# Binary cross entropy of 8192x8192 on one core: a side block of 24 rows, loaded by part of the DMA engines at launch and near the end, and chunks of 13824 columns

## The chip, the core and the metric

The kernel runs on one core of one Trainium2 chip. The core has several engines that run their own instruction streams: VectorE (DVE in the profile), ScalarE (ACT), GpSimd (POOL), SyncE (SP) and TensorE (PE, which has no work here). Sixteen DMA engines move data between HBM and the on-chip memory of 128 partitions. Transfers are issued by SP or by POOL; the profile lists SP's as queue q1 (hardware_dynamic) and POOL's as q0 (software_dynamic).

The metric is the time of one execution on the device in microseconds (us). The kernel before takes 1865.45 us, the median of three runs (1865.32 to 1865.6).

## The reference

```python
def reference(pred, target):                     # both 8192 x 8192, float32
    eps = 1e-7
    pred = np.clip(pred, eps, 1 - eps)
    return -(target * np.log(pred) + (1 - target) * np.log(1 - pred))
```

The predictions lie between 0.01 and 0.99. The target is 0 or 1 in every element, so the result is -log|target - 1 + pred|: for target 1 this is -log(pred), for target 0 it is -log(1 - pred). The kernel computes it in that form. Two arrays of 268 MB are read from HBM and one of 268 MB is written.

## The kernel before, in words

The three arrays are taken as flat and cut into chunks. A chunk of w columns is 128 x w consecutive elements, one partition holding w of them. The 524288 columns are cut by `plan` into two chunks of 5120 (`FIRST`), 35 of 14336 (`BIG`), two of 5632 (`LAST`) and one of 1024 (`TAIL`): 40 chunks.

Two tiles hold the data. `ring_p` (float32) has three slots of `BIG` columns and a place for the last chunk; pred is loaded into it, everything is computed in place, and the result is stored from it. `ring_t` (bf16) has one slot of `BIG` columns and a place for the last chunk; the target is loaded into it by a transfer that casts float32 to bf16. As there is one slot, the target of chunk k+1 can be loaded only when DVE has read all of the target of chunk k.

The work on a chunk, in halves for the large ones, is:

- `clip` (L80): DVE, tensor_scalar, clamps pred to [eps, 1-eps]
- `log`: first DVE (L86, scalar_tensor_tensor: target - 1 + pred), then ACT twice (L89 absolute value, L90 logarithm)
- `back` (L94): DVE, tensor_scalar, times -1
- `store` (L76): a transfer from `ring_p` to the output

`load_p` (L69) and `load_t` (L72) are issued on POOL, as are the stores, with these exceptions on SP: the pred load of chunk 0, and the stores of the last three chunks. One transfer of a chunk has 128 rows, one for each partition. Each DMA engine takes eight of them, one after the other, and works through what has been issued in the order of its queues.

The order is written out by hand (`tc.manual_schedule`), and each engine runs its instructions in that order. At launch POOL issues the target loads of chunks 0 and 1 and the pred loads of chunks 1 and 2, SP the pred load of chunk 0. After DVE has worked on chunks 0 and 1, POOL issues the target load of chunk 2, then the stores of chunks 0 and 1 and the pred load of chunk 3. From then on one round of the loop over k computes chunk k, issues the target load of chunk k+1 (when the second L86 of chunk k is done), the store of chunk k (when the second L94 is done), and the pred load of chunk k+2. The last three chunks are interleaved by hand.

The semaphores are put in by the framework from the data that instructions touch. POOL's transfers use eight semaphores in turn, so that a transfer of POOL also waits until the one issued eight before it has landed.

Of the kernel before, what the change touches and what calls it, by code (L numbers as in the profile page):

```python
# [1 line left out]

# [4 lines left out]

EPS = 1e-7

BIG = 14 * 1024  # L10
FIRST = 5 * 1024
LAST = 5632
TAIL = 1024
SLOTS = 3


def plan(total):
    n = (total - 2 * FIRST - 2 * LAST - TAIL) // BIG
    assert n > 4 and total == 2 * FIRST + n * BIG + 2 * LAST + TAIL
    spots = [(FIRST, 0, 0), (FIRST, FIRST, FIRST)]  # L20
    spots += [(BIG, k % SLOTS * BIG, 0) for k in range(1, n + 1)]
    end = (n + 1) % SLOTS * BIG
    spots += [(LAST, end, 0), (LAST, end + LAST, LAST)]
    return spots + [(TAIL, SLOTS * BIG, BIG)]


@with_exitstack
def kernel(
    ctx: ExitStack,
    tc: tile.TileContext,  # L30
    pred: bass.AP,
    target: bass.AP,
    out: bass.AP,
):
    nc = tc.nc
    fp32 = mybir.dt.float32
    bf16 = mybir.dt.bfloat16
    Alu = mybir.AluOpType
    Act = mybir.ActivationFunctionType
    P = nc.NUM_PARTITIONS  # L40

    R, C = pred.shape
    spots = plan(R * C // P)
    n = len(spots)
    widths = [s[0] for s in spots]
    cols = [sum(widths[:k]) for k in range(n)]

    def chunk(ap, k):
        flat = ap.rearrange("r c -> (r c)")
        return flat[cols[k] * P : (cols[k] + widths[k]) * P].rearrange("(p w) -> p w", p=P)  # L50

    pool = ctx.enter_context(tc.tile_pool(name="rings", bufs=1))
    ring_p = pool.tile([P, SLOTS * BIG + TAIL], fp32, name="ring_p", tag="ring_p")
    ring_t = pool.tile([P, BIG + TAIL], bf16, name="ring_t", tag="ring_t")
    warm = pool.tile([1, 8], fp32, name="warm", tag="warm")

    def spot(k, part=(0, 1)):
        w, c, _ = spots[k]
        i, m = part
        return ring_p[:, c + i * w // m : c + (i + 1) * w // m]  # L60

    def spot_t(k, part=(0, 1)):
        w, _, c = spots[k]
        i, m = part
        return ring_t[:, c + i * w // m : c + (i + 1) * w // m]

    def load_p(k):
        queue = nc.sync if k == 0 else nc.gpsimd
        queue.dma_start(out=spot(k), in_=chunk(pred, k))  # L69

    def load_t(k):
        nc.gpsimd.dma_start(out=spot_t(k), in_=chunk(target, k))  # L72

    def store(k):
        queue = nc.sync if k >= n - 3 else nc.gpsimd
        queue.dma_start(out=chunk(out, k), in_=spot(k))  # L76

    def clip(k, *part):
        p = spot(k, *part)
        nc.vector.tensor_scalar(  # L80
            out=p, in0=p, scalar1=EPS, scalar2=1 - EPS, op0=Alu.max, op1=Alu.min
        )

    def log(k, *part):
        p = spot(k, *part)
        nc.vector.scalar_tensor_tensor(  # L86
            out=p, in0=spot_t(k, *part), scalar=1.0, in1=p, op0=Alu.subtract, op1=Alu.add
        )
        nc.scalar.activation(out=p, in_=p, func=Act.Abs)  # L89
        nc.scalar.activation(out=p, in_=p, func=Act.Ln)  # L90

    def back(k, *part):
        p = spot(k, *part)
        nc.vector.tensor_scalar(out=p, in0=p, scalar1=-1.0, scalar2=None, op0=Alu.mult)  # L94

    with tc.manual_schedule():
        nc.vector.memset(warm, 1.0)  # L97
        load_t(0)
        load_p(0)
        load_t(1)  # L100
        load_p(1)
        load_p(2)
        nc.scalar.activation(out=warm, in_=warm, func=Act.Ln)  # L103
        for k in (0, 1):
            clip(k)
            log(k)
        load_t(2)
        back(0)
        store(0)
        back(1)  # L110
        store(1)
        load_p(3)
        a, b, c = range(n - 3, n)
        for k in range(2, n - 3):
            for h in (0, 1):
                clip(k, (h, 2))
                log(k, (h, 2))
            if k < n - 4:
                load_t(k + 1)
            else:  # L120
                load_t(a)
                load_t(b)
                load_p(c)
                load_t(c)
                back(k, (0, 2))
                for j in (a, b):
                    clip(j)
            if k < n - 4:
                back(k, (0, 2))
            back(k, (1, 2))  # L130
            store(k)
            if k + 2 < n - 3:
                load_p(k + 2)
            elif k + 2 == n - 3:
                load_p(a)
                load_p(b)
        log(a, (0, 2))
        log(a, (1, 2))
        clip(c)
        log(b, (0, 2))  # L140
        back(a, (0, 2))
        log(b, (1, 2))
        back(a, (1, 2))
        store(a)
        log(c)
        back(b, (0, 2))
        back(b, (1, 2))
        store(b)
        back(c)
        store(c)  # L150


# [1 line left out]
_INS = ['pred', 'target']  # L154
_OUTS = [((8192, 8192), 'float32')]


# [23 lines left out]
```

## Time and profile before

| what | before |
|---|---|
| median of three runs | 1865.45 us |
| the profiled execution | 1865.98 us |
| its span, first to last instruction | 1864.2 us |
| DVE busy | 1121.5 us (60%) |
| ACT busy | 902.4 us (48%) |
| POOL busy | 178.4 us (10%) |
| HBM read, written | 536.87 MB, 268.44 MB |
| L86 on 128x7168, 70 times | 7.625 us each |
| L89, L90 on 128x7168, 70 times each | 6.17, 6.18 us each |
| L80, L94 on 128x7168, 70 times each | 3.89 us each |
| L72 on POOL waits for DVE's L86 | 1057.4 us in all, 37 times |
| L86 on DVE waits for the target's transfer | 371.9 us in all, 35 times |
| large target load, issue to landing | 31.3 us (median of 35) |
| large pred load, issue to landing | 44.3 us (median of 35) |
| large store, issue to landing | 31.1 us (median of 35) |

Times of instructions are from the start of the span. An engine's busy time is the sum of its instructions; the profile puts the idle time ahead of an instruction down to what ended it. The DMA share of a stretch is the mean over the sixteen DMA engines; in short stretches it can come out a few per cent above 1 or below the true share. The profile has no number for a DMA engine, but it has the start and length of every packet, and packets that follow each other without a gap can be joined into sixteen chains. "Target chunk 2" and the like count chunks from 0, as `k` does.

### The profile page before, as it was taken

The page shows a single profiled execution, that of the slowest core. Times are in us where ns is not written, and L with a number is a line of the kernel's source. Part 1 is how long each engine was busy: PE and PEld are TensorE (multiplying, and loading weights), DVE is VectorE, ACT ScalarE, POOL GpSimd, SP SyncE. Part 2 cuts the span into 40 slices and gives each one's busy share as a digit, 9 for nine tenths or more (in the row PEclk, how much of TensorE's full clock was granted, in tenths as well). Part 3 has the DMA queues.
Part 4 walks back from the last instruction along what each step waited for, and adds up shares of the span by engine and source line. Part 5 has one row for each costly group of instructions (what it writes and reads, how often), then busy time and mean ns, then how long its engine had stood idle before and what let it go on. Part 6 is the DMA issues. An engine that isn't in the chain of part 4 may idle for free.

```text
span 1864.2 us, 704 instructions
## 1 busy us (share of the span) xinstructions
DVE 1121.5 (60%) x230; ACT 902.4 (48%) x156; POOL 178.4 (10%) x120
## 2 busy tenths in 40 slices
DVE  4666555555666566555555666566655555666565
ACT  4454444455555544444455555544444445555554
POOL 1111101111110011101111110011101111110020
DMA  9999999999999999999999999999999999999999
GB/s 345 346 371 356 354 354 353 354 354 356 357 374 373 375 372 354 354 354 356 359 356 359 357 368 375 376 373 362 353 354 354 356 354 354 356 367 374 374 357 348
DMA packets 17286, 671.15 MB, mean 360 GB/s; under 512 B 1920, under 2 KB 1920, under 8 KB 2304
## 3 DMA queue, kind: packets, MB, share of 16 engines
q0 software_dynamic: 16704, 662.18, 99.0%
q1 hardware_dynamic: 576, 8.91, 1.1%
q14 instruction: 6, 0.05, 0.0%
HBM read 536.87 MB, written 268.44 MB: 432 GB/s over the span
## 4 chain that ended last, share of the span: by engine, by line
DMA 60%; issue 35%; ACT 3%; DVE 2%; POOL 0%; POOLq 0%; DVEq 0%; PEldq 0%
DMA ring_t<-in_target_dram 57%; DMA ring_p<-in_pred_dram 4%; ACT ring_p L90 1%; ACT ring_p L89 1%; DVE ring_p L86 1%; DVE ring_p L94 0%; DVE ring_p L80 0%; POOL out_dram L76 0%; POOL ring_t L72 0%; POOLq L72 0%; POOL ring_p L69 0%; POOLq L76 0%; DVEq L86 0%; PEldq L176 0%
## 5 line engine op out<-in xcount | busy, mean ns | idle before, releaser
L89 ACT ACTIVATE ring_p<-ring_p 128x7168 f32<-128x7168 f32 (+3 forms) x77 | 452.0, 5870 | 942.7 <-DVE ring_p L86 942.7
L86 DVE SCALAR_TENSOR_TENSOR ring_p<-ring_t,ring_p 128x7168 f32<-128x7168 bf16 (+3 forms) x77 | 558.2, 7251 | 373.2 <-DMA ring_t<-in_target_dram 371.9
L94 DVE TENSOR_SCALAR ring_p<-ring_p 128x7168 f32<-128x7168 f32 (+3 forms) x77 | 285.4, 3706 | 329.5 <-ACT ring_p L90 329.5
L90 ACT ACTIVATE ring_p<-ring_p 128x7168 f32<-128x7168 f32 (+3 forms) x77 | 452.6, 5877 | 2.5
L80 DVE TENSOR_SCALAR ring_p<-ring_p 128x7168 f32<-128x7168 f32 (+3 forms) x75 | 284.5, 3794 | 23.9 <-DMA ring_p<-in_pred_dram 23.9
L76 POOL DMA_DIRECT2D out_dram<-ring_p x37 | 127.9, 3458 | 584.5 <-DVE ring_p L94 584.3
L72 POOL DMA_DIRECT2D ring_t<-in_target_dram x40 | 28.9, 722 | 1058.2 <-DVE ring_p L86 1057.4
L69 POOL DMA_DIRECT2D ring_p<-in_pred_dram x39 | 21.7, 558 | 2.5 <-issue 2.5
L103 ACT ACT_TABLE_LOAD x1 | 1.3, 1283 | 0.7 <-PEq L165 0.7
L97 DVE MEMSET warm<- 1x8 f32 x1 | 0.1, 65 | 0.8 <-PEq L165 0.8
L103 ACT ACTIVATE warm<-warm 1x8 f32<-1x8 f32 x1 | 0.2, 208 | 0.0
L165 POOL MEMSET const-float32-0.0<- 128x1 f32 x1 | 0.1, 98 | 0.2 <-issue 0.2
L165 POOL MEMSET const-bfloat16-1.0<- 128x1 bf16 x1 | 0.1, 101 | 0.0
L165 POOL MEMSET const-float32-1.0<- 128x1 f32 x1 | 0.1, 98 | 0.0
L165 POOL MEMSET const-uint8-127<- 128x1 uint8 x1 | 0.1, 98 | 0.0
## 6 DMA issues: line engine op xcount, KB each, us to landing
ring_p<-in_pred_dram POOLq DMA_DIRECT2D x35, 7168.0 KB, 44.3
out_dram<-ring_p POOLq DMA_DIRECT2D x35, 7168.0 KB, 31.1
ring_t<-in_target_dram POOLq DMA_DIRECT2D x35, 3584.0 KB, 31.3
ring_p<-in_pred_dram POOLq DMA_DIRECT2D x2, 2816.0 KB, 37.2
out_dram<-ring_p SPq DMA_DIRECT2D x2, 2816.0 KB, 14.7
out_dram<-ring_p POOLq DMA_DIRECT2D x2, 2560.0 KB, 28.7
ring_t<-in_target_dram POOLq DMA_DIRECT2D x2, 1408.0 KB, 26.5
ring_p<-in_pred_dram SPq DMA_DIRECT2D x1, 2560.0 KB, 13.0
```

The costliest lines, as they stand in the source:

```text
L69: queue.dma_start(out=spot(k), in_=chunk(pred, k))
L72: nc.gpsimd.dma_start(out=spot_t(k), in_=chunk(target, k))
L76: queue.dma_start(out=chunk(out, k), in_=spot(k))
L80: nc.vector.tensor_scalar(out=p, in0=p, scalar1=EPS, scalar2=1 - EPS, op0=Alu.max, op1=Alu.min)
L86: nc.vector.scalar_tensor_tensor(out=p, in0=spot_t(k, *part), scalar=1.0, in1=p, op0=Alu.subtract, op1=Alu.add)
L89: nc.scalar.activation(out=p, in_=p, func=Act.Abs)
L90: nc.scalar.activation(out=p, in_=p, func=Act.Ln)
L94: nc.vector.tensor_scalar(out=p, in0=p, scalar1=-1.0, scalar2=None, op0=Alu.mult)
L97: nc.vector.memset(warm, 1.0)
L103: nc.scalar.activation(out=warm, in_=warm, func=Act.Ln)
L165: nc = _bacc.Bacc("TRN2", target_bir_lowering=False, num_devices=1)
```

## The change

The sizes of the chunks change: 36 chunks of 13824 columns (not 35 of 14336), two first ones of 6912 (not 5120), two of 5632 as before, and a last one of 948 (not 1024). The remaining 588 columns' worth of data, 75264 elements of each array, form a side block in two tiles of their own, `side_p` and `side_t`, both float32.

The side block has a low and a high part. The low part is 24 rows of 2x800 elements, in groups of 12, 8 and 4 rows (`GROUPS`). Its target and pred are loaded by six transfers that SP issues at launch, behind the pred load of chunk 0. The high part is the complement: 4, 8 and 12 rows (16 less the group) of 2x768 elements. POOL loads its target at k = n-13 and its pred at k = n-12, and stores the result at k = n-8. The low part's result is computed at k = 4 and stored by POOL in three pieces of 384, 384 and 32 columns at k = n-13, n-12 and n-8. Here n is the number of chunks, 41. Each group has the partitions j, j+9, j+18 and so on for the low part, and 3+j, 12+j and so on for the high one, so that no partition is shared.

Both parts are computed by DVE and ACT on all 128 partitions of the side tiles, 1600 columns at k = 4 and 1536 at k = n-9, with the same five operations as a chunk. Two memsets of DVE fill the side tiles at launch, so that partitions that no transfer fills hold numbers.

```diff
--- before.py
+++ after.py
@@ -7,16 +7,20 @@
 
 EPS = 1e-7
 
-BIG = 14 * 1024
-FIRST = 5 * 1024
+BIG = 108 * 128
+FIRST = BIG // 2
 LAST = 5632
-TAIL = 1024
+TAIL = 948
 SLOTS = 3
+HALF = 800
+CUT = 768
+GROUPS = [12, 8, 4]
+SIDE = 24 * 2 * (HALF + CUT) // 128
 
 
 def plan(total):
-    n = (total - 2 * FIRST - 2 * LAST - TAIL) // BIG
-    assert n > 4 and total == 2 * FIRST + n * BIG + 2 * LAST + TAIL
+    n = (total - 2 * FIRST - 2 * LAST - TAIL - SIDE) // BIG
+    assert n > 12 and total == 2 * FIRST + n * BIG + 2 * LAST + TAIL + SIDE
     spots = [(FIRST, 0, 0), (FIRST, FIRST, FIRST)]
     spots += [(BIG, k % SLOTS * BIG, 0) for k in range(1, n + 1)]
     end = (n + 1) % SLOTS * BIG
@@ -52,7 +56,29 @@
     pool = ctx.enter_context(tc.tile_pool(name="rings", bufs=1))
     ring_p = pool.tile([P, SLOTS * BIG + TAIL], fp32, name="ring_p", tag="ring_p")
     ring_t = pool.tile([P, BIG + TAIL], bf16, name="ring_t", tag="ring_t")
+    side_p = pool.tile([P, 2, HALF], fp32, name="side_p", tag="side_p")
+    side_t = pool.tile([P, 2, HALF], fp32, name="side_t", tag="side_t")
     warm = pool.tile([1, 8], fp32, name="warm", tag="warm")
+    low_cols = sum(widths) * P
+    high_cols = low_cols + sum(GROUPS) * 2 * HALF
+
+    def low(ap, j, a, b):
+        flat = ap.rearrange("r c -> (r c)")
+        at = low_cols + sum(GROUPS[:j]) * 2 * HALF
+        block = flat[at : at + GROUPS[j] * 2 * HALF]
+        return block.rearrange("(h p w) -> p h w", h=2, w=HALF)[:, :, a:b]
+
+    def low_rows(tile_, j, a, b):
+        return tile_[j : j + 9 * GROUPS[j] - 8 : 9, :, a:b]
+
+    def high(ap, j):
+        flat = ap.rearrange("r c -> (r c)")
+        at = high_cols + sum(16 - g for g in GROUPS[:j]) * 2 * CUT
+        block = flat[at : at + (16 - GROUPS[j]) * 2 * CUT]
+        return block.rearrange("(h p w) -> p h w", h=2, w=CUT)
+
+    def high_rows(tile_, j):
+        return tile_[3 + j : 3 + j + 9 * (16 - GROUPS[j]) - 8 : 9, :, 0:CUT]
 
     def spot(k, part=(0, 1)):
         w, c, _ = spots[k]
@@ -93,10 +119,44 @@
         p = spot(k, *part)
         nc.vector.tensor_scalar(out=p, in0=p, scalar1=-1.0, scalar2=None, op0=Alu.mult)
 
+    def load_low():
+        for j in range(len(GROUPS)):
+            for tile_, ap in ((side_t, target), (side_p, pred)):
+                nc.sync.dma_start(
+                    out=low_rows(tile_, j, 0, HALF), in_=low(ap, j, 0, HALF)
+                )
+
+    def store_low(j, a, b):
+        nc.gpsimd.dma_start(out=low(out, j, a, b), in_=low_rows(side_p, j, a, b))
+
+    def load_high(tile_, ap, j):
+        nc.gpsimd.dma_start(out=high_rows(tile_, j), in_=high(ap, j))
+
+    def store_high(j):
+        nc.gpsimd.dma_start(out=high(out, j), in_=high_rows(side_p, j))
+
+    def compute_side(w):
+        p = side_p[:, :, 0:w]
+        nc.vector.tensor_scalar(
+            out=p, in0=p, scalar1=EPS, scalar2=1 - EPS, op0=Alu.max, op1=Alu.min
+        )
+        nc.vector.scalar_tensor_tensor(
+            out=p, in0=side_t[:, :, 0:w], scalar=1.0, in1=p, op0=Alu.subtract, op1=Alu.add
+        )
+        nc.scalar.activation(out=p, in_=p, func=Act.Abs)
+        nc.scalar.activation(out=p, in_=p, func=Act.Ln)
+
+    def finish_side(w):
+        p = side_p[:, :, 0:w]
+        nc.vector.tensor_scalar(out=p, in0=p, scalar1=-1.0, scalar2=None, op0=Alu.mult)
+
     with tc.manual_schedule():
         nc.vector.memset(warm, 1.0)
+        nc.vector.memset(side_t, 0.0)
+        nc.vector.memset(side_p, 0.5)
         load_t(0)
         load_p(0)
+        load_low()
         load_t(1)
         load_p(1)
         load_p(2)
@@ -115,6 +175,10 @@
             for h in (0, 1):
                 clip(k, (h, 2))
                 log(k, (h, 2))
+            if k == 4:
+                compute_side(HALF)
+            elif k == n - 9:
+                compute_side(CUT)
             if k < n - 4:
                 load_t(k + 1)
             else:
@@ -128,9 +192,23 @@
             if k < n - 4:
                 back(k, (0, 2))
             back(k, (1, 2))
+            if k == 4:
+                finish_side(HALF)
+            elif k == n - 9:
+                finish_side(CUT)
             store(k)
             if k + 2 < n - 3:
                 load_p(k + 2)
+                for j in range(len(GROUPS)):
+                    if k == n - 13:
+                        store_low(j, 0, CUT // 2)
+                        load_high(side_t, target, j)
+                    elif k == n - 12:
+                        store_low(j, CUT // 2, CUT)
+                        load_high(side_p, pred, j)
+                    elif k == n - 8:
+                        store_low(j, CUT, HALF)
+                        store_high(j)
             elif k + 2 == n - 3:
                 load_p(a)
                 load_p(b)
```

## The prediction

> **What bounds the kernel now.** I read the page's head first, then busy time by stretch, then the DMA queues at launch, then the time line of DVE and POOL around the first large target load.
>
> The page, its busy engines, slices and bytes:
>
> ```profile
> span 1864.2 us, 704 instructions
> DVE 1121.5 (60%) x230; ACT 902.4 (48%) x156; POOL 178.4 (10%) x120
> DMA  9999999999999999999999999999999999999999
> HBM read 536.87 MB, written 268.44 MB: 432 GB/s over the span
> ```
>
> Busy time by stretch (length, then DVE, ACT, POOL, the granted clock, the DMA share, GB/s):
>
> ```profile
> 4.00:26.00 22.00, 8.32 (x2) 3.82 (x1) 0.00 (x0) 1.00 1.01 310
> 26.00:43.50 17.50, 11.05 (x3) 11.93 (x4) 3.10 (x2) 1.00 1.01 435
> 60.00:1850.00 1790.00, 1095.45 (x222) 882.98 (x150) 168.71 (x108) 1.00 1.00 362
> 1859.00:1860.00 1.00, 0.00 (x0) 0.00 (x0) 0.00 (x0) 1.00 0.66 272
> 1860.00:1862.00 2.00, 0.00 (x0) 0.00 (x0) 0.00 (x0) 1.00 0.25 102
> 1862.00:1863.10 1.10, 0.00 (x0) 0.00 (x0) 0.00 (x0) 1.00 0.07 26
> ```
>
> The sixteen DMA engines are the bound: their share is 1.00 for 1790 us while DVE has 40% and ACT 52% spare. Whatever DVE or ACT gains or loses is worth nothing unless an engine runs dry. The end is uneven: from 1860 to 1862 a quarter of the engines (four) still work, from 1862 to 1863.1 one. An even end would save 0.34x1 + 0.75x2 + 0.93x1.1 = 2.9 us, no more.
>
> The trace's single packets give the price of a row (one partition's line). From start to start 57344 bytes take 2.114 us, 22528 take 0.833, 20480 take 0.758: 5 ns plus bytes at 27.2 per ns; a target row (cast to bf16) takes 14 ns more; a transfer's closing packet 6 to 19 ns. Twelve engines begin at 1.74 to 1.95 us, three at 2.5 to 2.6, one at 3.6. Engines 0 to 4.5 us out of step in mid-run all show the same 2.114: a row is as quick out of step as in step.
>
> DMA queues in two stretches of the launch, 1.7 to 5.2 us (first line) and 5.2 to 5.9 (the other two):
>
> ```profile
> q1 hardware_dynamic: 59, 1.21, 96.8%
> ...
> q0 software_dynamic: 11, 0.11, 76.1%
> q1 hardware_dynamic: 5, 0.10, 34.0%
> ```
>
> POOL issued its first load at 1.24 and was through with it at about 1.8, yet q0 (POOL's queue) moves nothing before 5.2: 3.4 us from issue to first packet.
>
> Time line, chunk 1's end and load of target chunk 2 ("t2"):
>
> ```profile
> 28.27 2.83 DVE L80 TENSOR_SCALAR ring_p<-ring_p 128x5120 f32<-128x5120 f32 x1 [6.13 <-DMA ring_p<-in_pred_dram]
> 31.13 5.49 DVE L86 SCALAR_TENSOR_TENSOR ring_p<-ring_t,ring_p 128x5120 f32<-128x5120 bf16 x1
> 36.54 2.82 DVE L94 TENSOR_SCALAR ring_p<-ring_p 128x5120 f32<-128x5120 f32 x1
> 36.92 2.57 POOL L72 DMA_DIRECT2D ring_t<-in_target_dram  x1 [33.43 <-DVE ring_p L86]
> 39.66 0.54 POOL L76 DMA_DIRECT2D out_dram<-ring_p  x1 [0.17 <-issue]
> ```
>
> t2 can be issued only when DVE has left chunk 1's target. Its issue, 0.53 us elsewhere, takes 2.57 here and ends 0.13 after L94 does: POOL is held while that DVE operation runs. Issued by 39.5, t2's first packet on the earliest engine comes at 43.5, right behind the last row of pred chunk 2, without a gap. So issue to first packet is at most 4.0, and this is the thinnest cover in the kernel.
>
> **The change, part by part.** The profiled execution took 1865.98 (span 1864.2 and 1.8 around it), 0.5 above the median 1865.45; I carry the difference over to the median. Its last data packet ends at 1863.0.
>
> *Bytes.* 524288 columns before and after: 2x6912 + 36x13824 + 2x5632 + 948 + 588. Nothing to gain at 27.2 bytes per ns.
>
> *One more chunk.* 41 triples of target load, pred load and store, not 40: 8 rows x (5+5+19 ns) and three closings, +0.26 us on every engine.
>
> *Packets of the side block.* An engine of the last group (none of the 24 low rows, three of the high ones) gets 18 packets x 5 ns and some 15 closings x 6 ns: +0.2 us. The first group gets 30 packets, six of them 128 bytes long; no such row exists, and between the 4-byte packet (9 ns) and the 2048-byte one (173 ns) these are 0.05 to 1.0 us. That group has less left to do after t2 (below), so I count 0.2.
>
> *Launch.* Two memsets of 128x1600 on DVE, from about 0.9: by L94's 1621 ns (2816 columns) and 693 (1024) 1.0 us each, by L86's at most 1.8. They may hold POOL's first issue till 2.9 (4.5). With the 3.4 us above q0 starts by 6.3 (7.9). Cover: SP's first pred load, 8 rows x 1.02 us from 1.74, to 10.4. Cost 0; past the cover, us for us. The six low loads wait on SP for the memsets behind that load; nothing is behind them but stores of the end.
>
> *t2.* Before it lie four chunk loads of 6912, not 5120 (32 rows x 0.2635 = +8.43 us), so pred chunk 2 starts on the earliest engine at 26.57 + 8.43 = 35.0 and its 8 rows of 2.038 end at 51.3. To this come an engine's own lateness (0 to 1.3) and its low rows: 1.5 us with three rows (12 packets of 3200 bytes, 123 ns, and closings), 1.0, 0.5, 0. Engines thus run dry at 51.9 to 53.5. Pred chunk 1 lands with the slowest, the first group: 35.0 + 1.5 + about 0.3 + 0.4 = 37.2. L80 then takes 3.8, L86 7.4 (7168 columns: 7.625): 48.4. Back(0) occupies DVE till 52.1, holding POOL as before; t2's issue ends at about 52.25. First packet: 0.6 us later if it is as quick as SP's (0.74+0.37 to 1.74), 4.0 at most. I take 3.4, the one row of this queue and operation: 55.65, so a gap of 2 to 3.7 us in which all sixteen engines run dry, and so lose both the new spacing and their old lateness. Queued behind on POOL is store(0); 16.4 us of t2 cover it.
>
> By the Trainium skill (DMA: Bandwidth & Descriptors, Specifications) a GpSimd transfer's first byte comes about 1 us after issue; the launch shows 3.4. By the page's figure t2 would start at 53.25 and the estimate would be 2.4 us lower than mine.
>
> *The stagger.* One low row with both inputs and both halves is 4 x 123 = 0.49 us, about a quarter of a 2.04 us row: groups of engines a quarter row apart. Price 0, since rows are equally quick out of step.
>
> *Side compute, at k = 4 and n-9.* DVE 1.0 + 1.8 + 1.0, ACT 2 x 1.5 (1024 columns: 1.04, 2816: 2.54). The last DVE operation waits for ACT, and the next chunk's clip queues behind it, 4 us late; then DVE waits 10.7 us for the target in any case. Cost 0, up to 4 us each without that cover.
>
> *POOL's side transfers.* 18 issues of 0.5 (3.6 when held) in three chunks, after a store and a pred load and ahead of the next target load, before which POOL idles 29 us. A transfer also waits until the eighth before it has landed: at n-13 POOL waits for the target chunk in flight, and the next target load for a store that lands some 18 us after it, just under the 19.4 us that DVE needs. Behind that, a target load lies 14 us in the queue (31.3 to landing, 17.0 of service). Cost 0.
>
> *Tail.* Loads and stores of 5632 stay; the last large store (the cover) is 0.6 us shorter, the compute under it 1.3 shorter. Cost 0.
>
> **Sum.** An engine without lateness takes 1815.8 us from t2's first packet (43.5) to its last one (1859.3). Afterwards 6656 columns more lie ahead of t2 (8 rows x 4 bytes / 27.2: -7.83), the last group's share is 0.04 smaller, and 0.46 is added: 1808.4. 55.65 + 1808.4 = 1864.05; engines that start alike drifted 0 to 0.7 apart before, I take 0.35: 1864.4, against 1863.0: +1.4 us. On the median: 1866.8.
>
> **The rivals.**
> *The cover holds nearly (SP-like latency).* t2 at 52.9 on the last groups: 1861.3, plus 0.35 to 1.5: -0.6, some 1864.8. For it: the launch may be a cold start. Against: no row.
> *Slower: late engines lose again.* Before, the engines that began late grew from 0.7-1.3 to 1.6-4.5 us late at the turns from target load to store, where their last target row took 0.2 to 0.6 us longer. If after the gap one engine grows 3.2 late again: 55.65 + 1808.4 + 3.2 = 1867.25, +4.2, 1869.7. It passes 0.2% (3.7 us; about what a measurement of this kernel can tell from no change) from 2.7 us of growth on. For it: the four late ones; against: after a common restart none is late.
> *Faster: spacing ends that loss.* Even end: -2.9; with +0.46, and at best the 1.2 us that all lost once at the end of t2's load: -2.4 to -3.7, 1861.7 to 1863.0. Against: the gap at t2, which takes the spacing away after 52 us.
> *The change doesn't do what it says.* If GpSimd's parts start at the first engine too, the first group has 4800 elements more after t2 than in the sum, 0.9 us with packets: 1867.7. The Trainium skill (same page, Why a DMA increments its semaphore by 16 and not by 1) has SP use the lowest-numbered engines and GpSimd a moving cursor, which would give the complement; no run here shows it.
>
> **How the numbers follow.** Forecast 0.43, nearly covered 0.22, late again 0.18, spacing helps 0.11, wrong engines 0.06. Slower by over 0.2%: 0.13 of late again, 0.04 of the wrong engines with a long gap: 0.17. Faster by over 0.2%: the far end of the fourth, 0.08. Within: 0.75. The range 1863.2 to 1869.4 leaves out that far end and the top of late again.
>
> **What would show it.** A DMA share below 1 at 52 to 56 us and t2's first packet some 3.4 us after its issue; an issue of about 3.5 us ended by back(0); row times unchanged in mid-run; DVE still waiting about 10 us for each target, also after k = 4 and n-9; the last engines ending closer together. Wrong if an engine runs dry at n-13 to n-8 or in the tail, if 12-row transfers load one engine, or if rows become slower or quicker when spaced.

## The result, and the profile after

The changed kernel takes 1869.89 us (median of 11 runs, 1868.69 to 1870.95), the kernel before 1865.6 us in the same series (11 runs, 1865.23 to 1866.15). The ratio is 1.0023, with a 95% interval of 1.0015 to 1.0031: slower by 4.3 us. The forecast was 1866.8 with a range to 1869.4, and "within 0.2%" as the likeliest case. The measured time lies above that range and just beyond 0.2%. A second series, on another occasion, gave 1870.72 against 1866.07.

The page of the changed kernel, its head:

```profile
span 1867.5 us, 773 instructions
DVE 1130.9 (61%) x244; ACT 907.8 (49%) x164; POOL 194.1 (10%) x141
...
HBM read 536.87 MB, written 268.44 MB: 431 GB/s over the span
```

The DMA engines are still the bound. This execution took 1869.25 us; its last data packet ends at 1865.8 us of the span, that of before at 1863.0. Busy time by stretch, first the two long ones, then four around the target load of chunk 2 ("t2"), then the end (length, DVE, ACT, POOL, granted clock, DMA share, GB/s):

```profile
26.00:43.50 17.50, 9.12 (x3) 11.93 (x2) 0.00 (x0) 1.00 1.03 426
60.00:1850.00 1790.00, 1100.03 (x235) 881.51 (x158) 187.62 (x131) 1.00 1.00 361
...
49.00:51.00 2.00, 2.00 (x1) 2.00 (x1) 2.00 (x1) 1.00 0.96 415
51.00:53.00 2.00, 1.36 (x1) 2.00 (x1) 1.83 (x2) 1.00 0.26 111
53.00:55.00 2.00, 0.00 (x0) 1.97 (x2) 0.19 (x1) 1.00 1.36 221
55.00:57.00 2.00, 0.00 (x0) 2.00 (x1) 0.00 (x0) 1.00 1.03 221
...
1860.00:1862.00 2.00, 0.00 (x0) 0.00 (x0) 0.00 (x0) 1.00 0.80 336
1862.00:1863.10 1.10, 0.00 (x0) 0.00 (x0) 0.00 (x0) 1.00 0.47 198
1863.10:1864.20 1.10, 0.00 (x0) 0.00 (x0) 0.00 (x0) 1.00 0.29 123
1864.20:1865.90 1.70, 0.00 (x0) 0.00 (x0) 0.00 (x0) 1.00 0.23 94
```

Two things are new. At 51 to 53 us the share falls to 0.26. (In stretches this short a row is counted where it begins, so the hole is in truth a little later: by the packets the engines finish pred chunk 2 between 51.7 and 53.4 us, and t2's first rows begin between 53.17 and 54.01.) And the end is longer: before, one engine worked on past 1862.2 us; here eight do, and six of them to 1865 us or later.

The time line of DVE and POOL ahead of the hole:

```profile
37.53 3.76 DVE L106 TENSOR_SCALAR ring_p<-ring_p 128x6912 f32<-128x6912 f32 x1 [8.35 <-DMA ring_p<-in_pred_dram]
41.33 7.36 DVE L112 SCALAR_TENSOR_TENSOR ring_p<-ring_t,ring_p 128x6912 f32<-128x6912 bf16 x1
48.60 3.75 DVE L120 TENSOR_SCALAR ring_p<-ring_p 128x6912 f32<-128x6912 f32 x1
48.98 3.50 POOL L98 DMA_DIRECT2D ring_t<-in_target_dram  x1 [45.47 <-DVE ring_p L112]
```

POOL's issue of t2 takes 3.50 us and ends at 52.48, 0.13 after the "times -1" (L120) that holds it. The first packet follows 0.70 us later, at 53.17.

Packets that follow each other on an engine show how far the sixteen engines are apart. The table gives, for one transfer at each of three places, by how many us each engine finishes after the first (from the packets of the two traces):

```
before  t2's load      0 .00 .01 .03 .09 .12 .12 .14 .25 .29 .30 .63 1.03 1.07 1.09 1.86
        near 970 us    0 .06 .09 .10 .11 .22 .26 .27 .30 .32 .63 .65 2.78 2.81 2.82 3.74
        last packets   0 .06 .09 .10 .11 .22 .26 .27 .62 .64 .72 1.31 2.78 2.82 2.88 3.74
changed t2's load      0 .03 .09 .12 .15 .18 .19 .28 .35 .55 .56 .77 .79 .90 .96 1.15
        near 1017 us   0 .04 .21 .27 .29 .30 .31 .39 .65 .78 2.68 2.76 3.14 3.40 3.49 3.72
        last packets   0 .04 .08 .26 .27 .29 .75 .75 1.24 1.30 3.61 3.69 3.81 4.09 4.23 4.40
```

Both kernels end up in two bunches, a prompt one and a late one 2.7 to 4.4 us behind: four late engines before, six afterwards. By the chains, the engines at the back of the field after t2's load, from some 0.6 to 1.0 us on, become the late bunch. They lose their time in one place, the last row of a target load, when stores come next: between 80 and 1790 us, 22 of the 25 slow packets before, and some 60 of 80 to 90 afterwards, are such last rows (0.44 us of 0.50 for a mean engine, and 1.05 of 1.25).

### The profile page after: what moved, and what is told of

Its sections match the earlier page's. It is cut to its first block, busy times and chain, and to the rows that moved or that the text cites. A ratio compares the mean times of both kernels' runs of the same rounds, so it can differ in the third digit from the quotient of the medians.

```text
span 1867.5 us, 773 instructions
## 1 busy us (share of the span) xinstructions
DVE 1130.9 (61%) x244; ACT 907.8 (49%) x164; POOL 194.1 (10%) x141
## 4 chain that ended last, share of the span: by engine, by line
DMA 59%; issue 33%; DVE 5%; ACT 2%; POOL 0%; POOLq 0%; DVEq 0%; PEldq 0%
DMA ring_t<-in_target_dram 55%; DMA ring_p<-in_pred_dram 4%; DVE ring_p L112 3%; ACT ring_p L116 1%; ACT ring_p L115 1%; DVE ring_p L106 1%; DVE ring_p L120 0%; POOL out_dram L102 0%; POOL ring_t L98 0%; POOL ring_p L95 0%; POOLq L98 0%; POOLq L102 0%; DVEq L112 0%; PEldq L254 0%
## 5 line engine op out<-in xcount | busy, mean ns | idle before, releaser
L115 ACT ACTIVATE ring_p<-ring_p 128x6912 f32<-128x6912 f32 (+2 forms) x79 | 451.8, 5719 | 940.5 <-DVE ring_p L112 940.5
L112 DVE SCALAR_TENSOR_TENSOR ring_p<-ring_t,ring_p 128x6912 f32<-128x6912 bf16 (+2 forms) x79 | 557.9, 7063 | 368.4 <-DMA ring_t<-in_target_dram 367.1
L120 DVE TENSOR_SCALAR ring_p<-ring_p 128x6912 f32<-128x6912 f32 (+2 forms) x79 | 285.3, 3612 | 324.4 <-ACT ring_p L116 324.4
L116 ACT ACTIVATE ring_p<-ring_p 128x6912 f32<-128x6912 f32 (+2 forms) x79 | 452.4, 5727 | 2.5
L106 DVE TENSOR_SCALAR ring_p<-ring_p 128x6912 f32<-128x6912 f32 (+2 forms) x77 | 284.6, 3696 | 27.2 <-DMA ring_p<-in_pred_dram 27.2
L102 POOL DMA_DIRECT2D out_dram<-ring_p x38 | 121.2, 3190 | 579.0 <-DVE ring_p L120 578.9
L95 POOL DMA_DIRECT2D ring_p<-in_pred_dram x40 | 30.9, 775 | 0.0
L130 POOL DMA_DIRECT2D out_dram<-side_p x9 | 5.2, 574 | 0.0
L147 ACT ACTIVATE side_p<-side_p 128x1600 f32<-128x1600 f32 (+1 forms) x2 | 3.0, 1510 | 0.1
L146 ACT ACTIVATE side_p<-side_p 128x1600 f32<-128x1600 f32 (+1 forms) x2 | 3.0, 1494 | 0.0
L136 POOL DMA_DIRECT2D out_dram<-side_p x3 | 1.7, 575 | 7.0 <-DMA ring_t<-in_target_dram 7.0
L151 DVE TENSOR_SCALAR side_p<-side_p 128x1600 f32<-128x1600 f32 (+1 forms) x2 | 1.9, 970 | 0.0
L140 DVE TENSOR_SCALAR side_p<-side_p 128x1600 f32<-128x1600 f32 (+1 forms) x2 | 1.9, 969 | 0.0
```

Of the source, the lines that this page charges most:

```text
L106: nc.vector.tensor_scalar(out=p, in0=p, scalar1=EPS, scalar2=1 - EPS, op0=Alu.max, op1=Alu.min)
L112: nc.vector.scalar_tensor_tensor(out=p, in0=spot_t(k, *part), scalar=1.0, in1=p, op0=Alu.subtract, op1=Alu.add)
L130: nc.gpsimd.dma_start(out=low(out, j, a, b), in_=low_rows(side_p, j, a, b))
```

## The experiments

Three theories were put against each other. GAP: the engines run dry ahead of t2's load, because its issue depends on DVE's work on chunk 1, which comes later with first chunks of 6912 columns and low rows ahead of them, and then on L120, which holds POOL. SPACING: the side block's uneven shares make engines late. CHUNKS: the sizes of the chunks do it. Unless told otherwise a kernel computes everything. Times are medians of 4 to 11 runs; ratios are to the kernel before, run beside it.

### The chunks alone

```diff
-BIG = 14 * 1024
-FIRST = 5 * 1024
+BIG = 108 * 128
+FIRST = BIG // 2
-TAIL = 1024
+TAIL = 1536
```

> The chunks of the changed kernel (13824 columns, first ones of 6912, a last one of 1536) without the side block; the whole of both arrays is computed. GAP (the engines run dry before the target load of chunk 2, because it is issued too late): the low rows no longer delay pred chunk 1, so the issue comes 1.2 to 1.5 us earlier and the dry time of the earliest engine shrinks from 1.5 us to about 0.4; time between before and changed, 1866.0 to 1867.0. SPACING (the side block's uneven shares put more engines late, and these lose time at every turn from target load to store): four late engines as in before, time within 0.7 us of before. CHUNKS (the loss comes from the new sizes themselves): 1868.5 to 1870, as changed.

1868.24 us, ratio 1.0014 (1.0005 to 1.0022). More than half of the loss comes without any side block, more than GAP's 1867. The issue of t2 is held here too:

```profile
47.64 3.50 POOL L72 DMA_DIRECT2D ring_t<-in_target_dram  x1 [44.14 <-DVE ring_p L86]
```

The engines finish pred chunk 2 from 51.3 us on, and t2 starts at 51.83, 0.70 us after the end of its issue: here too a hole, half a microsecond on the earliest engine.

### The changed kernel without the gap

```diff
         load_t(2)
+        same(0, 900)    # scalar_tensor_tensor: max(1*p, p) on chunk 0's first 900 columns
         back(0)
```

> The changed kernel with one added DVE operation of about 1 us (chunk 0's first 900 columns replaced by the larger of themselves and themselves) ahead of the first times -1, so that POOL's issue of target chunk 2 is not held by the times -1 (issue 0.5 us, not 3.5, first packet near 50.2 us, not 53.1). GAP: no engine runs dry at 51 to 53 us and the time falls by 1.5 to 2.5 us, to 1867.4 to 1868.4. SPACING: no gap, but more engines late than the six of the changed kernel, since the quarter-row spacing now survives; the time stays at 1869 to 1871. CHUNKS: 1868.5 to 1870.

1867.65 us, ratio 1.0011 (1.0002 to 1.0020): 2.2 us below the changed kernel, as GAP has it. It was run again, beside the changed kernel:

> The changed kernel itself, beside the next three on one chip: 1869 to 1871.

> The changed kernel with the added DVE operation that frees the issue of target chunk 2, again. GAP: 1.5 to 2.8 us below the changed kernel of this series. If the first difference of 2.2 us was chance: within 0.7 us of it.

1870.72 and 1868.14 us: 2.6 us. The time line of the second:

```profile
48.69 1.09 DVE L124 SCALAR_TENSOR_TENSOR ring_p<-ring_p 128x900 f32<-128x900 f32 x1
48.80 5.96 ACT L115 ACTIVATE ring_p<-ring_p 128x6912 f32<-128x6912 f32 x1 [7.78 <-DVE ring_p L112]
49.06 0.53 POOL L98 DMA_DIRECT2D ring_t<-in_target_dram  x1 [45.55 <-DVE ring_p L112]
49.81 3.76 DVE L120 TENSOR_SCALAR ring_p<-ring_p 128x6912 f32<-128x6912 f32 x1
```

The issue takes 0.53 us, as it runs beside a scalar_tensor_tensor and is over when L120 begins. DVE has 1.1 us more to do, and the kernel is 2.6 us faster. The stretches of the same run show no hole:

```profile
49.00:51.00 2.00, 1.97 (x2) 2.00 (x1) 0.53 (x1) 1.00 0.96 415
51.00:53.00 2.00, 2.00 (x1) 2.00 (x1) 0.00 (x0) 1.00 1.06 318
53.00:55.00 2.00, 0.57 (x1) 1.97 (x2) 0.54 (x1) 1.00 0.97 207
```

What the gap cost can be followed row by row, for the mean engine. In the changed kernel it waits 0.85 us; in the first of these two runs it doesn't. The first row of t2 is 0.57 us shorter without the gap, and the last one 0.83. The late engines remain, as SPACING had it: eight are 1.9 to 4.9 us behind at their last packets in the first run (six, 2.7 to 4.6, in the second), and the slow rows after 80 us cost 0.45 us more than with the gap. So with these chunks engines become late without a gap too: the field is as spread out (4.85 us, 4.40 with it), but the first engine ends 2.0 us earlier (1859.46, not 1861.42).

### A longer gap

```diff
             clip(k)
+            if k == 1:
+                same(1, 2700)
             log(k)
         load_t(2)
```

> The changed kernel with one DVE operation of about 3 us (the first 2700 columns of chunk 1 replaced by the larger of themselves and themselves) ahead of chunk 1's scalar_tensor_tensor, so that target chunk 2 starts 3 us later, near 56.1 us. GAP: 2.5 to 3.5 us above the changed kernel, as all engines now wait the whole 3 us more. Chance or spread alone: under 1 us above it.

1873.57 us, 2.85 above the changed kernel of the same series, ratio 1.0039 (1.0026 to 1.0051). The added operation took 2.97 us:

```profile
41.40 2.97 DVE L124 SCALAR_TENSOR_TENSOR ring_p<-ring_p 128x2700 f32<-128x2700 f32 x1
...
52.05 3.50 POOL L98 DMA_DIRECT2D ring_t<-in_target_dram  x1 [48.54 <-DVE ring_p L112]
```

Once the engines are dry, DVE time ahead of this issue is kernel time: here 2.97 us of it cost 2.85.

### A gap in the kernel before

```diff
             clip(k)
+            if k == 1:
+                same(1, 4500)
             log(k)
```

> The kernel before with one added DVE operation of about 5 us (chunk 1's first 4500 columns replaced by the larger of themselves and themselves) ahead of chunk 1's first scalar_tensor_tensor, so that target chunk 2 is issued 5 us later and its first packet comes near 45.2 us, where the engines run dry at 43.5 to 44.8. GAP (a dry spell here costs its own length, the slow first rows after it, and the spread that it leaves): 1.0 to 2.5 us over before, as the changed kernel lost 2.2 to it. SPACING or CHUNKS (the gap as such costs little): under 0.5 us over before.

1869.04 us against 1865.89, ratio 1.0017 (1.0008 to 1.0026): 3.15 us more, above GAP's 2.5. The time line and the stretches:

```profile
31.23 4.85 DVE L98 SCALAR_TENSOR_TENSOR ring_p<-ring_p 128x4500 f32<-128x4500 f32 x1
...
41.89 2.57 POOL L72 DMA_DIRECT2D ring_t<-in_target_dram  x1 [38.40 <-DVE ring_p L86]
```

```profile
43.00:45.00 2.00, 1.34 (x1) 2.00 (x1) 1.83 (x2) 1.00 0.00 0
45.00:47.00 2.00, 0.00 (x0) 1.97 (x2) 0.17 (x1) 1.00 1.44 229
```

The kernel before has no hole there:

```profile
43.00:45.00 2.00, 0.00 (x0) 2.00 (x1) 0.00 (x0) 1.00 1.07 229
```

The issue ends at 44.46, the first packet comes at 45.17, and the mean engine starts t2 1.5 us later than before's. The kernel pays twice that. The first rows after the hole are slower, by 0.8 us for the mean engine, and the slow rows after 80 us cost it 0.6 more; the late engines are fewer (three) but later (one by 4.8 us in mid-run).

### The chunks alone without the gap, and the side block on the old chunks

The first has the edits of the chunks alone and `same(0, 900)`. The second:

```diff
-BIG = 108 * 128
-FIRST = BIG // 2
-TAIL = 948
+BIG = 14 * 1024
+FIRST = 5 * 1024
+TAIL = 730
-HALF = 800
-CUT = 768
+HALF = 400
+CUT = 384
```

> The chunks alone, as in the first of these, with the added DVE operation of the second, so that nothing holds the issue of target chunk 2. GAP: no dry time, 1865.3 to 1866.3, up to 0.7 us below the chunks alone. SPACING: within 0.7 us of before, whatever the gap. CHUNKS: 1868.5 to 1870.

> The side block at half its width (2x400 and 2x384 columns, an eighth of a row of spacing) on the chunks of before (14336, first ones of 5120, a last one of 730). The full width does not fit beside these chunks. GAP: before has 2.5 us or more of cover at the target load of chunk 2 and the low rows take 0.75 of it; no gap, time within 1 us of before plus 0.4 for packets: 1865.5 to 1866.6. SPACING: more late engines than the four of before, 1867 to 1869. CHUNKS: as before, 1865.5 to 1866.6.

Both take 1867.04 us; the ratios 1.0008 (0.9999 to 1.0016) and 1.0007 (0.9998 to 1.0016) reach to no change. The first is 1.2 us below the chunks alone, so these too lost to the gap, more than the 0.7 expected; against CHUNKS, some 1.3 us is left for the sizes themselves. The trace of the first shows where it goes: it has no gap, yet six engines end 2.7 to 4.8 us late, and slow rows after 80 us cost the mean engine 1.24 us, where before has 0.49. The second lost 1.3 us, between what GAP and SPACING had for it; its trace has no gap, four engines 2.1 to 3.5 us late in mid-run and a fifth 1.3, and 0.3 us more of ordinary packet time.

With the gap closed, side block and spacing together cost 0.6 us (1867.65 less 1867.04), of which their packets are more than half: counted from start to start at their ordinary length, all packets of a mean engine add up to 1855.8 us before, 1856.0 with the new chunks, and 1856.3 with the side block. On the old chunks half a side block cost 1.3 us, so its price is not the same everywhere, and why is open.

### The pred load ahead of the store

```diff
-            store(k)
             if k + 2 < n - 3:
                 load_p(k + 2)
+            store(k)
```

It was made in the kernel before, in the changed kernel without the gap, and in the changed kernel:

> The kernel before with the pred load of chunk k+2 issued ahead of the store of chunk k, so that the engines turn from target load to pred load and from pred load to store. TURN (late engines lose 0.2 to 0.6 us at each turn from a target row to a store, until they are more than a row late): engines stay within about 2 us of each other through mid-run, the last ends closer to the others, time 0.5 to 2.5 us below before. NOT TURN (the growth comes with any turn to a store, or with lateness alone): the same four to six engines 2.7 to 4 us late, time within 0.7 us of before.

> The changed kernel with the added DVE operation that removes the gap (1867.65 by itself) and with the pred load ahead of the store. TURN: 0.5 to 2.5 us below 1867.65. NOT TURN: within 0.7 us of 1867.65.

> The changed kernel with the pred load ahead of the store, the gap left in. TURN: the six late engines don't form; 1 to 3 us below 1869.89, so that what is left over before is the gap (about 1.5 us) and the packets (about 0.5 us). NOT TURN: within 0.7 us of 1869.89.

1870.52, 1871.59 and 1875.40 us: 4.6, 3.9 and 5.5 us more than without the swap (the second and third against an earlier series). TURN's remedy falls. What the packets show is that the loss moved with the store: in the kernel before with the swap, a mean engine loses about 1.7 us in the last rows of pred loads (some 90 slow ones), which now come ahead of the stores, and 0.1 in those of target loads. And it grows on: five engines are 4.4 to 6.6 us late near 1325 us, where the other order is still below 5. Why the one order grows further is open. In the last of the three the engines also run dry near the end (a DMA share of 0.73 from 1720 to 1725 us and 0.78 from 1850 to 1855), so its 5.5 us are not all of this kind.

### All stores on SP

```diff
-        queue = nc.sync if k >= n - 3 else nc.gpsimd
+        queue = nc.sync
```

> The kernel before with all stores issued by SP, so that stores and loads lie in two queues of each engine and mix row by row, with no turn from a target load to a store. TURN (lateness grows at such turns): the last ends lie within 2 us of each other, 1 to 3 us below before, 1863 to 1865. Otherwise: the four late engines stay, or the target loads come later behind mixed rows; 1865 to 1869.

2137.95 us, ratio 1.1455. This says nothing on the turns, since the edit did more than it was meant to. POOL, without the stores, comes to the next pred load at once and waits there until an older store has landed, with the next target load queued behind it:

```profile
L69 POOL DMA_DIRECT2D ring_p<-in_pred_dram x39 | 133.2, 3416 | 381.8 <-DMA out_dram<-ring_p 381.8
...
ring_p<-in_pred_dram POOLq DMA_DIRECT2D x35, 7168.0 KB, 53.2
out_dram<-ring_p SPq DMA_DIRECT2D x35, 7168.0 KB, 41.7
```

Stores mixed with loads land in 41.7 us, not 31.1, and the engines run dry in mid-run, as in this stretch:

```profile
320.00:330.00 10.00, 9.01 (x2) 9.97 (x3) 3.47 (x2) 1.00 0.31 57
```

## Why the prediction was wrong

**The gap: forecast, and there.** That the engines run dry ahead of t2, and why, was right: pred chunk 1 was at DVE at 37.5 (forecast 37.2), L120 held POOL till 52.48 (52.25), the engines ran dry from 51.7 to 53.4 (51.9 to 53.5). Taking the gap out gives back 2.2 to 2.6 of the 4.3 to 4.7 us, making it longer costs the added time, and putting one into the kernel before costs 3.15.

**The latency was mis-sized.** "I take 3.4, the one row of this queue and operation": it was 0.70 in the changed kernel and 0.70 to 0.71 in the five other runs in which the engines were dry. The launch was no measure of it; the low bound (0.6, from SP's row) came close. That put t2's start 2.5 us too late, at 55.65 and not 53.17. By the rival "the cover holds nearly", a start this early should have given 1864.8.

**The step that failed: a common restart as a clean start.** "Engines that start alike drifted 0 to 0.7 apart before, I take 0.35." The 0.7 was read off the engines that were prompt anyway. After the restart the engines were 0 to 0.83 us apart, 1.15 after t2's load, and six of them then went through the growth that I had kept for a rival: the last packets are 4.4 us apart. That is 4.05 us more than the sum had. With these chunks the growth needs no gap: in the three kernels without one the last packets are 4.6 to 4.9 us apart. What starts it stays open. The rival "late engines lose again" had the mechanism, and its 1869.7 is close to the result, but it put t2 2.5 us too late as well, so the agreement is partly chance.

**A term left out, and one too large.** First rows after a dry spell are slower (0.66 us for the mean engine in the changed kernel, none before). The 128-byte pieces travel in pairs, 18 ns a pair, below the 0.05 to 1.0 us that six of them were given. From t2's first packet to the end of the engine that finishes first it is 1808.25 us, where the sum has 1808.4; the traces don't show that this is one engine, so the agreement may be chance.

**Readings that were off.** The 14 ns of a cast row are its length, not its cost: such rows overlap, and from start to start one of 14336 columns takes 2.112 us, no more than a plain one (2.114). So the new chunk cost 0.15 us, not 0.26. The side block's packets cost the mean engine more than the 0.2 (0.3 to 0.4), so the 0.46 for both came out right (0.45) by luck. Before, the late engines grew to 2.8 to 3.7 us, not to 1.6 to 4.5, and nothing was 4.5 out of step.

**The two sums.** For the last packet: 1864.4 forecast, less 2.5 for the latency, plus 4.05 for the late engines, is 1865.95; the trace has 1865.8. From there to the median the forecast missed another 1.7 us: the time between the last packet and the end of the execution was 3.43 us and not 2.96, and this profiled execution lay 0.6 below its median where the one before had lain 0.5 above.

**What the mean engine lost.** It ends at 1863.2 us and not 1860.3. Of these 2.9 us, 0.45 is packets, 0.85 the dry wait, 0.65 the slow first rows and 0.85 slow rows later on, nearly all of them last rows; the launch and what is left make up the other 0.1.

**What held.** Row times out of step were unchanged. The rival "spacing ends that loss" falls too: with the gap closed the spacing survives t2's load, and the slow rows after 80 us cost the mean engine 1.7 us, where the new chunks alone lose 1.24. The side compute was free: DVE still waits for the targets (367 us in 36 waits). POOL's side transfers were free: it waited 6.9 to 7.7 us for the target in flight, as worked out, and the next target load still had to wait for DVE:

```profile
1396.88 0.56 POOL L133 DMA_DIRECT2D side_t<-in_target_dram  x1 [6.88 <-DMA ring_t<-in_target_dram]
1415.40 0.57 POOL L98 DMA_DIRECT2D ring_t<-in_target_dram  x1 [17.96 <-DVE ring_p L112]
```

The launch memsets took 1.39 us each and didn't hold POOL, whose two issues beside them took 1.21 us. The rival "wrong engines" was not settled: the side block's short packets mix up the chains by which engines are told apart. With 0.6 us for the whole side block once the gap is closed, it probably didn't cost much.

**What stays open.** Of the 1.3 us that the sizes of the chunks cost without the gap, 0.15 is packets; most of the rest goes with the two more late engines, and why they become late is not known. How many engines become late differs from trace to trace (three to eight), and the traces don't tell which; only the place of the loss was shown, not its cause.

## What to carry to other kernels

In a kernel that is bound by transfers, look for the place where the queue is shortest before touching sizes; here it was the first load after the start-up block, with 3 us to spare, and larger chunks and the side block's rows ahead of it used them up. A hole there cost two to three times the mean engine's wait (0.44, 0.85 and 1.5 us in three kernels), in part because the first rows after it are slow. Engines that fall behind one another are a loss of their own: it was there with the hole and without it. Where POOL must issue a transfer just as DVE comes free, keep an operation that holds POOL out of that moment: 1.1 us of other DVE work put in between saved 2.2 to 2.6 us.

## What the runs showed of the hardware that I had not expected

- From the end of POOL's issue to the first packet it takes 0.70 to 0.71 us once the kernel runs (holes in six runs), against 3.4 us at launch. The Trainium skill (DMA: Bandwidth & Descriptors, Specifications) gives about 1 us, nearer to the measured than the launch row was.
- The first target rows after a hole of 0.85 us for the mean engine take 2.26 to 3.30 us where later ones take 2.06.
- An engine that is late when the others turn to stores loses up to 0.95 us in its last load row (changed kernel), again and again. With target, store, pred as the order of transfers the sixteen stayed within 5 us of each other until 1390 us in every kernel and ended 3.7 to 5.5 us apart; with target, pred, store they came to be 7.7 to 9.9 us apart.
